# The routed experts in plain float32 matmuls on two column halves of the array, with six more weight buffers

## The chip, the cores and the metric

The kernel runs on one core of one Trainium2 chip, as one program. The metric is the device time of that core in microseconds. The core has a tensor engine (PE, with its weight loads shown apart as PEld), a vector engine (DVE), a scalar engine (ACT), a general engine (POOL), a queue that only issues transfers (SP), and 16 DMA engines. On PE a product has a stationary operand, which is loaded first, and a moving operand, which is streamed through the array column by column.

## What is computed

The reference is a network of two blocks on 512 tokens of width 1024, with a mixture of experts at its end. The change touches the experts alone. There are 32 of them, each token goes to two, and an expert is a gated layer with a hidden width of 512:

```python
N_EXPERTS = 32; TOP_K = 2; D_FF_EXPERT = 512; D_MODEL = 1024
# for every expert e, for the tokens t that the router sent to it:
xn = rms_norm(t, norm_gain)
h  = silu(xn @ w_gate[e]) * (xn @ w_up[e])      # 1024 -> 512
y  = h @ w_down[e]                               # 512 -> 1024
# a token's output: the sum over its two experts, weighted by the router
```

Everything is float32. The weights of one expert are three matrices of 2 MB, and all 32 experts are read whatever the routing says, which is 201 MB.

## The kernel before

The program is one long list of tile operations, emitted by Python methods of a class `Net` and put in order on each engine by a planner. `layer1` runs twice, then `mix2`, `cross` and `moe`. The change is in `moe`, the last phase.

Matmuls are made of a split: a float32 operand is written as a high and a low part of a reduced type (float32r), by one ACT copy and one DVE subtraction (`split`, L258 and L259), and a product is then three passes, high by high, high by low and low by high (`mm3`, L282 to L284). The expert phase does it too.

In `moe` the router fills, for each expert, a list of up to 64 tokens (`CAP`). A loop over the 32 experts then does this:

- `gather` (L1485): POOL issues an indirect transfer that brings the rows of the expert's tokens to `xg`, one token per partition. There are two `xg`, and the next expert's gather is issued an expert ahead.
- `front` (L1489): eight PE transposes of `xg` into PSUM (L1493), a DVE product with the norm's gain (`ex`), a split of that (`exh`, `exl`), and then gate and up. Each is a sum over eight blocks of 128 rows, into a bank of its own (pools `mm` and `fmm`), of which the 64 partitions of the tokens are used. The tokens are the stationary operand (128 x 64), the weights the moving one (128 x 512). ACT forms the silu, and scales by the token's 1/rms (L1511); DVE multiplies by the up part (`esg`, L1512).
- `back` (L1515), one expert behind: four transposes of `esg` (L1520), a split (`ehh`, `ehl`), and the last product into two banks `S`, one per half of the 1024 columns. ACT copies both to `ey` (L1532) and POOL issues an indirect store to `y_d` (L1533).

The weights come through `weights` (L1470): tiles of 128 x 1024 float32 (512 KB), twelve per expert, in 34 buffers named `ew` that are used in turn. SP issues the transfers (L1475) in program order. The first use of each of the first 34 buffers is held back by a tiny POOL copy (`gate`, L249), so that the loads start at five points of the phases before: ten at `first`, up to sixteen at `early`, up to 24 at `late`, up to 32 once 1/rms is there, and the last two at `ready`, when the lists are made. Each tile is then split into `ewh` and `ewl`, with three buffers each.

After the loop four tiles `ew` receive the residual by tokens (L1557), POOL builds diagonal matrices `dg`, and SP loads the experts' rows `yt` from `y_d` (L1604), which waits for the last store. The sums, the last norm and the output follow.

Of the kernel before, what the change touches and what calls it, by code (L numbers as in the profile page):

```python
# [8 lines left out]
F32 = mybir.dt.float32  # L9
# [11 lines left out]
            hh=22, hl=22, gt=10, sq=2, fw=2, fwh=2, fwl=2, yh=8, yl=8, mgh=8, mgl=8, MKH=4, MKL=4, yt=4, xt=4, ew=34, ew1=16, ew2=24, ew3=32, xgs=2, ewh=3, ewl=3, exh=2, exl=2, esg=2, ex=2, ehh=2, ehl=2, ey=3, fs=4, fo=4)  # L21
# steps of a layer of the first block, see Net.layer1
ORDER = "P0 L0 A0 V0 O0 O1 W0 K0 Q0 Q1 C0 H0 H1 H2 H3 K1 Q2 Q3 C1 H4 H5 H6 H7 R0 R1"
T = 512
# [4 lines left out]
CAP = 64  # L29
NEG = -1.0e30  # L30

# ---------------------------------------------------------------- host layout
# Constants that depend on shapes alone, and inputs rearranged (no arithmetic).
# [5 lines left out]
def _constants():  # L39
# [56 lines left out]
    # what the last phase needs comes first  # L96
# [10 lines left out]
def _masks():  # L107
    """[128, 3, 128]: causal mask, strictly earlier rows, identity; and the forget rows' selectors"""
    p = np.arange(128)
    m = np.zeros((128, 10, 128), np.float32)  # L110
    m[:, 0] = np.where(p[None, :] > p[:, None], NEG, 0.0)
    m[:, 1] = p[:, None] < p[None, :]
    for h in range(8):
        m[h, 2 + h] = 1.0
        m[32 + h, 2 + h] = 1.0
    return m
# [41 lines left out]
def _chunks(w, starts, size=128):  # L158
    """[K, N] -> per chunk [128, K/128 * size]: the blocks of a column chunk, K blocks in order."""
    k = w.shape[0] // 128  # L160
    return np.stack([w[:, s:s + size].reshape(k, 128, size).transpose(1, 0, 2).reshape(128, k * size) for s in starts])


def _flat(w, width=1024):
    """[n, 128, W] -> tiles of `width` columns of the row of blocks."""
    a = w.transpose(1, 0, 2).reshape(128, -1)
    return np.ascontiguousarray(a.reshape(128, -1, width).transpose(1, 0, 2))
# [59 lines left out]
# ---------------------------------------------------------------- the kernel  # L227


class Net:  # L230
# [3 lines left out]
    # ---- small helpers  # L234
# [4 lines left out]
    def column(self, n):  # L239
        """a few columns of their own, for the whole program"""  # L240
        self.ncol += n
        return self.cols[:, self.ncol - n:self.ncol]

    def after(self, t, gate):
        """t's first write comes after `gate` is there."""
# [8 lines left out]
    def split(self, hi, lo, src, scale=None):  # L254
        """hi + lo = src (* scale per partition), both float32r."""
# [8 lines left out]
    def wload(self, ap, width, lane=""):  # L264
        """weights in two parts; lane f: buffers of their own, for products that fill other phases' gaps"""
# [12 lines left out]
    def mm3(self, ps, wst, wmv, first, last):  # L278
        """ps += (h + l of stationary)(h + l of moving), three passes."""
# [30 lines left out]
    def wstream(self, ap, lane=""):  # L310
        """blocks [128, 128] of tiles ap[n][128, 1024] in order."""
# [7 lines left out]
    def chunk(self, stream, xs, n=512, out=None):  # L319
        """one column chunk of 128 outputs: W^T x, x a list of (hi, lo)."""  # L320
# [5 lines left out]
    # ---- norm: x * gain in two parts, and 1/rms apart  # L326
# [26 lines left out]
    def sums(self, ps, sq, ones, nb, w=1, rows=slice(0, 128)):  # L353
        """column sums of sq [.., nb * 128] by token: ps[:, (b w)] = sq_b^T ones"""
# [3 lines left out]
    def rows(self, r):  # L358
        """columns r[t, i] as rows [i, t] of a scratch in memory"""
# [11 lines left out]
    def spread_pe(self, ps, r, nb, rows=128, stride=1, at=0):  # L371
        """ps[:rows, (b t)] = r[t, b], the same in every partition"""
# [6 lines left out]
    def spread(self, out, d, nb, at=0, stride=1):  # L379
        """out[p, (b t)] = row b of d, the same in every partition"""  # L380
# [4 lines left out]
    def rsqrt(self, out, ms, scale, eps):  # L385
        """out = (ms * scale + eps) ** -0.5 on a few columns: first guess from the bits, three Newton steps."""
# [16 lines left out]
    def tokens(self, ap, ntile, kper, n, xs, rtok, nb, evac, lane=""):  # L403
        """token-major projection: out[b] [128 tokens, n], W [128, kper, n] tiles."""
# [12 lines left out]
    def half_silu(self, out, ps, rstd):  # L417
        """out = silu(ps * rstd) as (tanh(z / 2) + 1) * z / 2"""
# [6 lines left out]
    # ---- q / k heads  # L425
    def rope(self, x, cos, sin, n=512):
        """x * cos + the other half of x * sin (signed), [128 (2 heads x 64), n]"""
# [10 lines left out]
    def head_sums(self, ps):  # L438
        """mean squares of raw heads by token: sums [128, (4 blocks, 2 heads)]"""
# [6 lines left out]
    def nsa_q(self, ps, gain, cos, sin, rtok):  # L446
        """raw roped q times gain as two stacks; per token and head rstd / 8."""
# [8 lines left out]
    def head_rsqrt(self, r, ms, rtok, scale, eps):  # L456
        """rtok * (rtok^2 * ms * scale + eps) ** -0.5 for [128, (4 blocks, 2 heads)]"""
# [30 lines left out]
    def q_stack(self, x, n=512):  # L488
        """heads of rows 0-63 and 64-127 -> two [hi; lo] stacks."""
# [10 lines left out]
    def k_stack(self, x, n=512, into=None):  # L500
        """per head [hi; hi] and [lo; lo]."""
# [16 lines left out]
    # ---- softmax rows  # L518
# [16 lines left out]
    def softmax_rows(self, Ps, scores, scale=None, gate=None):  # L535
        """of the four query blocks: exp(scale * (S - max)) * gate / row sum"""
# [20 lines left out]
    def softmax(self, P, S, n, scale=None):  # L557
        """exp(scale * (S - max)), its row sum's reciprocal."""
# [11 lines left out]
    def transposed(self, Ps, causal=True, two=True):  # L570
        """P of the four query blocks -> per key block ((hi, lo) or the whole, first query column)."""
# [28 lines left out]
    def values(self, n, name, two):  # L600
        """two: per head of 64 its two parts side by side"""
# [11 lines left out]
    def pv(self, out, v, p, first, last):  # L613
        """two parts: rows 0-63 high part of v times p, rows 64-127 low part of v times the high part of p"""
# [12 lines left out]
    def out_heads(self, O, row0, hi, lo):  # L627
        """O psum [64, 512] -> rows row0.. of the chunk's hi / lo."""
# [10 lines left out]
    # ---- block 1  # L639
# [37 lines left out]
    def compress(self, l, n):  # L677
        """the compressed keys [hi; hi], [lo; lo] of [128, (g 32)], and values per head."""
# [3 lines left out]
        for i, s in enumerate("kv"):  # L682
# [10 lines left out]
            # the 32nd block does not exist: its column is never used  # L693
# [73 lines left out]
    def cmp_probs(self, l, n, g):  # L767
# [4 lines left out]
        for qb in range(4):  # L772
# [18 lines left out]
            if qb == 0:  # L791
                # queries before the first whole block see none
# [6 lines left out]
    def nsa_head(self, l, n, h, hi, lo):  # L799
        """one query head: the three branches, gated, summed in one bank."""  # L800
# [16 lines left out]
    def hgrn_proj(self, l, xs, rstd):  # L817
        """log forget gates, keys and queries of the two pairs of heads."""
# [27 lines left out]
    def hgrn_levels(self, l, r):  # L846
        """A[s, t] = sum_d q_t k_s exp(b_t - b_s), s <= t, built over halved spans, two heads at a time.

        c: sums of log f from a span's start to t; e: log k_s plus the sum after s to its span's end.
        A's block of 128 rows sb lies at column 512 * sb, from its diagonal block on."""  # L850
# [106 lines left out]
    def residual(self, w, xs, then=None, lane=""):  # L957
        """h += W^T x"""
# [67 lines left out]
    # ---- block 2  # L1026
    def rope_tables(self):
        """cos and sin of positions * frequency, over the first block's tables."""
# [24 lines left out]
    def forget_rows(self, xs, rstd):  # L1053
        """minus the cumulated log forget gate per head, hi rows 0-7 and lo rows 32-39."""
# [17 lines left out]
        # log1p(e) = log(u) + (e - (u - 1)) / u  # L1072
# [107 lines left out]
    def gates(self, i, xs, rstd, lane=""):  # L1180
        """tanh(gate / 2)"""
# [8 lines left out]
    def branch(self, i, ys, ts, out, lane=""):  # L1190
        """out(m, tanh(gate / 2), y @ w_branch)"""
# [35 lines left out]
    def memory(self, gate):  # L1227
        """keys and values of the memory."""
# [67 lines left out]
    def router_chunk(self, k):  # L1296
        """squares and logits of a chunk of the residual: the logits' rows from the unscaled tokens"""
# [7 lines left out]
        if k % 4 == 3:  # L1305
            # the residual by tokens
# [9 lines left out]
    def moe(self, out):  # L1316
        nc, tc = self.nc, self.tc
        # per place (rank * experts + expert): the token, the row of its result (2 * token + choice), the token's 1/rms
# [4 lines left out]
        # small things: `keep` for the whole phase, `once` for the routing alone  # L1323
# [37 lines left out]
        # norm, routing: logits scaled by token  # L1361
# [15 lines left out]
        def onehot(oh, v, m, down, n):  # L1377
            """first place of the maximum"""
# [19 lines left out]
        # rank of each assignment within its expert, and its row among all sorted by expert  # L1398
# [14 lines left out]
        # lists of the first round: [place, (row, 1/rms), expert], out of bounds where there is none  # L1413
# [19 lines left out]
        # weights of the two experts  # L1433
# [10 lines left out]
        # all places, for further rounds  # L1444
# [24 lines left out]
        # experts  # L1469
        def weights(ap):  # L1470
# [5 lines left out]
            wh = self.tile([128, 1024], F32R, name="ewh")  # L1476
            wl = self.tile([128, 1024], F32R, name="ewl")
            if self.nw <= CAPS["ewh"]:
                self.gate(wh, rt)
                self.gate(wl, ready)  # L1480
            self.split(wh, wl, w)
            return wh, wl
# [5 lines left out]

        def front(xg, li_e, wg, wu, pool="mm"):  # L1489
            """the tokens of one place per partition through an expert's gate"""  # L1490
# [3 lines left out]
            xh = self.tile([128, 8, CAP], F32R, name="exh")  # L1494
            xl = self.tile([128, 8, CAP], F32R, name="exl")
            f3 = "p a b -> p (a b)"
            x = self.tile([128, 8, CAP], F32, name="ex")
            self.tt(x, pt.rearrange("p (k n) -> p k n", k=8), self.p("g_ffn")[:, :, None].to_broadcast([128, 8, CAP]), OP.mult)
            self.split(xh.rearrange(f3), xl.rearrange(f3), x.rearrange(f3))
            pss = []  # L1500
            for w3 in (wg, wu):
                ps = self.mmT(pool)[:CAP]
                for t in range(4):
                    wh, wl = weights(w3[:, 2 * t:2 * t + 2, :])
                    for kk in range(2):
                        k = 2 * t + kk
                        ws = slice(kk * 512, kk * 512 + 512)
                        self.mm3(ps, (xh[:, k, :], xl[:, k, :]), (wh[:, ws], wl[:, ws]), k == 0, k == 7)
                pss.append(ps)
            sg = self.tile([CAP, 512], F32, name="esg")  # L1510
            nc.scalar.activation(sg, pss[0], AF.Silu, scale=li_e[2])  # L1511
            nc.vector.scalar_tensor_tensor(sg, pss[1], li_e[2], sg, op0=OP.mult, op1=OP.mult)  # L1512
            return sg

        def back(sg, li_e, wd):  # L1515
            """the hidden rows through an expert's last product, to their rows of y_d"""
# [181 lines left out]
```

## Time and profile before

| | us |
|---|---|
| median of 3 runs | 2651.53 |
| runs | 2646.52 to 2654.74 |
| span of the profiled execution | 2651.4 |

| engine | busy us | share of the span |
|---|---|---|
| PE | 2582.3 | 97% |
| PEld | 1862.6 | 70% |
| DVE | 1816.4 | 69% |
| ACT | 1334.6 | 50% |
| POOL | 134.4 | 5% |

The profile has the span of one execution, the busy time of each engine, and the share of time in which the 16 DMA engines had packets under way. A record of PE spans from the start of a matmul to the modelled end of its results, so neighbouring records overlap; what a matmul costs in a row of matmuls is the distance from one start to the next. A plain float32 matmul stands in the trace as two records of the full number of columns.

The expert phase takes the last quarter of the span. Its first load is issued at 1950 us, its first matmul starts at 2038.66 and its last one at 2619.37.

### The profile page before, as it was taken

Reading aid. Unit: us, or ns where it says so; the run is one execution under the profiler, and the core shown is the slowest. Engines: PE = TensorE matmul, PEld = TensorE weight load, DVE = VectorE, ACT = ScalarE, POOL = GpSimd, SP = SyncE. Lnnn points to the kernel's source line nnn. Section 1 sums busy time; section 2 is a strip of 40 time slices with the busy share of each in tenths; the row PEclk is TensorE's granted clock in tenths of the full one; section 3 lists DMA queues with packets and bytes.
Section 4 is the critical chain, followed back from the end, with each engine's and each line's share of the span. In section 5 each row is a group of like instructions: output and inputs, shape, how many; then the busy total and the mean of one; then the engine's idle time right before and its main releaser. Section 6 shows DMA issues by size and latency. Waiting matters only on the chain. (4 is left out here: it accounts for less than half of the span.)

```text
span 2651.4 us, 33625 instructions
## 1 busy us (share of the span) xinstructions
PE 2582.3 (97%) x12098; PEld 1862.6 (70%) x12099; DVE 1816.4 (69%) x3496; ACT 1334.6 (50%) x2026; POOL 134.4 (5%) x199
## 2 busy tenths in 40 slices
PE   8999999999999999999999999999997999999997
PEld 6876557888888875678888877777874555555553
DVE  6778875444346888864443378677665989888986
ACT  6544553222235445442222256554443777877784
POOL 0000000000000000000000000000011110111102
PEclk9999999999999999999999999999997999999998
DMA  5132002222231231012222231222246999999996
GB/s 199 42 106 78 9 17 90 93 95 96 96 126 58 65 118 34 1 64 95 93 92 96 95 115 56 84 92 83 92 175 237 329 342 344 338 348 350 338 344 244
DMA packets 144316, 382.32 MB, mean 144 GB/s; under 512 B 15744, under 2 KB 16144, under 8 KB 143504
## 3 DMA queue, kind: packets, MB, share of 16 engines
q1 hardware_dynamic: 138160, 369.62, 41.0%
q0 software_dynamic: 5120, 8.40, 1.0%
q10 hardware_dynamic: 864, 2.10, 0.3%
q8 instruction: 96, 1.57, 0.2%
q14 instruction: 76, 0.62, 0.1%
HBM read 370.61 MB, written 12.59 MB: 145 GB/s over the span
## 5 line engine op out<-in xcount | busy, mean ns | idle before, releaser
L258 ACT ACTIVATE wh<-w 128x1024 fp32r<-128x1024 f32 (+1 forms) x264 | 276.5, 1048 | 642.8 <-PE mm L283 352.0
L282 PE MATMUL mm<-xh,wh 128*128 128x512 f32 x1232 | 494.7, 402 | 9.9 <-ACT wh L258 9.9
L283 PE MATMUL mm<-xl,wh 128*128 128x512 f32 x1232 | 493.7, 401 | 0.0
L284 PE MATMUL mm<-xh,wl 128*128 128x512 f32 x1232 | 491.3, 399 | 0.7 <-DVE wl L259 0.7
L259 DVE TENSOR_TENSOR ewl<-ew,ewh 128x1024 fp32r<-128x1024 f32 x384 | 450.8, 1221 | 50.5 <-ACT ewh L258 48.1
L259 DVE TENSOR_TENSOR wl<-w,wh 128x1024 fp32r<-128x1024 f32 (+1 forms) x264 | 319.6, 1211 | 172.8 <-ACT wh L258 171.6
L258 ACT ACTIVATE ewh<-ew 128x1024 fp32r<-128x1024 f32 x384 | 377.8, 1047 | 14.3 <-PE mm L284 5.1
L282 PEld LDWEIGHTS mm<-xh,wh 128*128 128x128 f32 x1232 | 232.8, 189 | 66.6 <-ACT wh L258 10.0
L283 PEld LDWEIGHTS mm<-xl,wh 128*128 128x128 f32 x1232 | 232.6, 189 | 55.5 <-issue 2.9
L284 PEld LDWEIGHTS mm<-xh,wl 128*128 128x128 f32 x1232 | 232.7, 189 | 54.0 <-DVE wl L259 1.5
L252 DVE TENSOR_TENSOR tmp<-mm,xrstd 128x512 f32<-128x512 f32 x104 | 71.6, 690 | 250.6 <-PE mm L284 244.1
L283 PE MATMUL mm<-hl,wh 128*128 128x512 f32 x352 | 138.6, 394 | 0.0
L282 PE MATMUL mm<-hh,wh 128*128 128x512 f32 x352 | 138.3, 393 | 0.0
L284 PE MATMUL mm<-hh,wl 128*128 128x512 f32 x352 | 138.2, 393 | 0.0
L549 ACT ACTIVATE P<-S,st,const 128x128 f32<-128x128 f32 (+3 forms) x128 | 78.5, 616 | 52.7 <-DVE st L252 43.0
L282 PE MATMUL mm<-ewh,exh 128*64 128x512 f32 x256 | 102.0, 398 | 1.8 <-ACT exh L258 1.8
L282 PE MATMUL S<-ewh,ehh 128*64 128x512 f32 x256 | 102.4, 400 | 1.0 <-ACT ehh L258 1.0
L283 PE MATMUL mm<-ewl,exh 128*64 128x512 f32 x256 | 102.5, 400 | 0.0
L284 PE MATMUL mm<-ewh,exl 128*64 128x512 f32 x256 | 101.8, 398 | 0.4 <-DVE exl L259 0.4
L283 PE MATMUL fmm<-ewl,exh 128*64 128x512 f32 x256 | 101.6, 397 | 0.0
L282 PE MATMUL fmm<-ewh,exh 128*64 128x512 f32 x256 | 100.6, 393 | 0.5 <-ACT ewh L258 0.5
L284 PE MATMUL fmm<-ewh,exl 128*64 128x512 f32 x256 | 100.6, 393 | 0.0
(514 smaller groups left out, 4779.7 us busy)
## 6 DMA issues: line engine op xcount, KB each, us to landing
ew<-in_eg_dram SPq DMA_DIRECT2D x128, 512.0 KB
ew<-in_eu_dram SPq DMA_DIRECT2D x128, 512.0 KB
ew<-in_ed_dram SPq DMA_DIRECT2D x128, 512.0 KB
w<-in_fi_dram SPq DMA_DIRECT2D x88, 512.0 KB
w<-in_w_dram SPq DMA_DIRECT2D x48, 512.0 KB
w<-in_fo_dram SPq DMA_DIRECT2D x44, 512.0 KB
w<-in_c_dram SPq DMA_DIRECT2D x16, 512.0 KB
tmp<-tmp SPq DMA_DIRECT2D x80, 64.0 KB
```

The source lines that it names most:

```text
L252: (eng or self.nc.vector).tensor_tensor(out, a, b, op=op)
L258: nc.scalar.activation(hi, src, AF.Copy)
L259: nc.vector.tensor_tensor(lo, src, hi.bitcast(F32), op=OP.subtract)
L282: nc.tensor.matmul(ps, ah, bh, start=first, stop=False)
L283: nc.tensor.matmul(ps, ah, bl, start=False, stop=False)
L284: nc.tensor.matmul(ps, al, bh, start=False, stop=last)
L549: nc.scalar.activation(Ps[q0 + i], S[:, :n], AF.Exp, bias=b, scale=1.0 if scale is None else scale[q0 + i], accum_out=st[:, 1, i:i + 1])
```

## The change

`weights` no longer splits: it returns the loaded float32 tile. The buffers `ewh`, `ewl`, `exh`, `exl`, `ehh`, `ehl` are gone, and `ew` has 40 buffers instead of 34; the gates of the first 32 stay, and the other eight are all held by `ready`. The products are single float32 matmuls. Gate goes to partitions 0 to 63 of one bank and up to partitions 64 to 127 of the same bank, so that they stand on the two column halves of the array, and the matmuls alternate between them; the two column halves of the last product do the same. 1/rms is now applied by an ACT copy to `xg` ahead of the transposes, instead of in the silu and in the product behind it. The weights of gate and up are asked for alternately.

```diff
-            hh=22, ..., ew=34, ew1=16, ew2=24, ew3=32, xgs=2, ewh=3, ewl=3, exh=2, exl=2, esg=2, ex=2, ehh=2, ehl=2, ey=3, fs=4, fo=4)
+            hh=22, ..., ew=40, ew1=16, ew2=24, ew3=32, xgs=2, esg=2, eh=2, ex=2, ehT=2, ey=3, fs=4, fo=4)
...
             nc.sync.dma_start(w.rearrange("p (a b) -> p a b", b=ap.shape[-1]), ap)
-            wh = self.tile([128, 1024], F32R, name="ewh")
-            wl = self.tile([128, 1024], F32R, name="ewl")
-            if self.nw <= CAPS["ewh"]:
-                self.gate(wh, rt)
-                self.gate(wl, ready)
-            self.split(wh, wl, w)
-            return wh, wl
+            return w
...
+        one, two_ = slice(0, CAP), slice(CAP, 2 * CAP)
+
         def front(xg, li_e, wg, wu, pool="mm"):
+            nc.scalar.activation(xg[:CAP], xg[:CAP], AF.Copy, scale=li_e[2])
             pt = self.mmT(self.ptn)
             for k in range(8):
                 nc.tensor.transpose(pt[:, k * 64:k * 64 + 64], xg[:CAP, k * 128:k * 128 + 128], self.c("ident")[:CAP, :CAP])
...
-            self.split(xh.rearrange(f3), xl.rearrange(f3), x.rearrange(f3))
-            pss = []
-            for w3 in (wg, wu):
-                ps = self.mmT(pool)[:CAP]
-                for t in range(4):
-                    wh, wl = weights(w3[:, 2 * t:2 * t + 2, :])
-                    for kk in range(2):
-                        k = 2 * t + kk
-                        ws = slice(kk * 512, kk * 512 + 512)
-                        self.mm3(ps, (xh[:, k, :], xl[:, k, :]), (wh[:, ws], wl[:, ws]), k == 0, k == 7)
-                pss.append(ps)
-            sg = self.tile([CAP, 512], F32, name="esg")
-            nc.scalar.activation(sg, pss[0], AF.Silu, scale=li_e[2])
-            nc.vector.scalar_tensor_tensor(sg, pss[1], li_e[2], sg, op0=OP.mult, op1=OP.mult)
-            return sg
+            ps = self.mmT(pool)
+            for t in range(4):
+                ws = [weights(w3[:, 2 * t:2 * t + 2, :]) for w3 in (wg, wu)]
+                for kk in range(2):
+                    k = 2 * t + kk
+                    for r, w in zip((one, two_), ws):
+                        nc.tensor.matmul(ps[r], x[:, k, :], w[:, kk * 512:kk * 512 + 512], start=k == 0, stop=k == 7)
+            sg = self.tile([128, 512], F32, name="esg")
+            nc.scalar.activation(sg[two_], ps[one], AF.Silu)
+            h = self.tile([CAP, 512], F32, name="eh")
+            self.tt(h, ps[two_], sg[two_], OP.mult)
+            return h
...
-            self.split(hh.rearrange(f3), hl.rearrange(f3), pt[:, :256])
-            py = [self.mmT("S")[:CAP] for _ in range(2)]
+            hT = self.tile([128, 4, CAP], F32, name="ehT")
+            nc.vector.tensor_copy(hT.rearrange(f3), pt[:, :256])
+            py = self.mmT("S")
             for k in range(4):
-                wh, wl = weights(wd[:, k:k + 1, :])
-                for half in range(2):
-                    ws = slice(half * 512, half * 512 + 512)
-                    self.mm3(py[half], (hh[:, k, :], hl[:, k, :]), (wh[:, ws], wl[:, ws]), k == 0, k == 3)
+                w = weights(wd[:, k:k + 1, :])
+                for i, r in enumerate((one, two_)):
+                    nc.tensor.matmul(py[r], hT[:, k, :], w[:, i * 512:i * 512 + 512], start=k == 0, stop=k == 3)
```

The rest of the diff takes comments out.

## Rows read from the trace of the kernel before

**Rows 1.** Stretches: length, busy us of five engines, granted PE clock, DMA share, GB/s.

```profile
2019.00:2035.00 16.00, 4.13 (x46) 3.94 (x46) 9.32 (x38) 3.15 (x5) 5.81 (x21) 0.50 0.77 276
2035.00:2045.00 10.00, 8.28 (x31) 4.95 (x32) 6.63 (x8) 2.96 (x4) 3.02 (x5) 0.51 0.73 235
2045.00:2100.00 55.00, 53.02 (x242) 30.19 (x241) 48.00 (x48) 44.03 (x51) 5.48 (x5) 1.00 0.94 322
2100.00:2350.00 250.00, 250.00 (x1169) 144.52 (x1168) 224.72 (x223) 197.59 (x237) 26.23 (x28) 1.00 0.97 339
2350.00:2590.00 240.00, 240.00 (x1126) 139.02 (x1125) 215.86 (x215) 190.07 (x227) 23.40 (x25) 1.00 0.99 346
2590.00:2603.00 13.00, 13.00 (x58) 7.38 (x57) 11.73 (x12) 10.64 (x14) 6.90 (x4) 1.00 0.98 363
```

**Rows 2.** Timeline of PE, one expert: start us, us, operation, records merged.

```profile
2300.70 0.66 PE L1493 MATMUL PU<-const,xg 64*128 64x64 f32 x8
...
2303.03 0.39 PE L283 MATMUL S<-ewl,ehh 128*64 128x512 f32 x1
2303.26 0.40 PE L284 MATMUL S<-ewh,ehl 128*64 128x512 f32 x1
2303.49 0.39 PE L282 MATMUL S<-ewh,ehh 128*64 128x512 f32 x1
...
2318.70 0.66 PE L1493 MATMUL PU<-const,xg 64*128 64x64 f32 x8
```

**Rows 3.** Instructions on tile `ew`, 2100 to 2600: count, ns min/median/max, starts.

```profile
L258 ACT ACTIVATE ewh<-ew x334: 1038/1046/1057, 2099.3 to 2599.5; 128x1024 fp32r<-128x1024 f32 x167
L259 DVE TENSOR_TENSOR ewl<-ew,ewh x333: 1207/1218/1310, 2099.7 to 2599.0; 128x1024 fp32r<-128x1024 f32 x167
L1475 SPq DMA_DIRECT2D ew<-in_ed_dram x108: 327/340/1076, 2108.7 to 2597.0; - x108
L1475 SPq DMA_DIRECT2D ew<-in_eu_dram x104: 367/368/1119, 2099.8 to 2582.1; - x104
L1475 SPq DMA_DIRECT2D ew<-in_eg_dram x100: 367/378/719, 2116.4 to 2579.1; - x100
```

**Rows 4.** Timelines of SP and PE where the experts begin.

```profile
2035.71 3.66 SPq L1475 DMA_DIRECT2D ew<-in_eg_dram  x3
...
2038.66 0.66 PE L282 MATMUL mm<-ewh,exh 128*64 128x512 f32 x1 [0.69 <-ACT exh L258]
```

**Rows 5.** Timelines of SP and PE at the end of the expert phase.

```profile
2593.25 4.81 SPq L1475 DMA_DIRECT2D ew<-in_ed_dram  x6
...
2619.37 0.40 PE L284 MATMUL S<-ewh,ehl 128*64 128x512 f32 x1
...
2626.14 1.99 SPq L1604 DMA_DIRECT2D yt<-y_d  x4
```

**Rows 6.** Timeline of PE: plain float32 matmuls one after another on one half.

```profile
1980.08 0.59 PE L1285 MATMUL O<-pth,memv 128*64 128x512 f32 x1
1980.51 0.59 PE L1285 MATMUL O<-pth,memv 128*64 128x512 f32 x1
1980.94 0.59 PE L1285 MATMUL O<-pth,memv 128*64 128x512 f32 x1
```

**Rows 7.** Timelines of DVE, PE and PEld: two plain float32 matmuls on both halves.

```profile
215.31 1.06 DVE L376 TENSOR_SCALAR tmp<-const 128x128 f32<-128x128 f32 x5
...
215.73 0.63 PE L377 MATMUL X<-tmp,const 128*64 128x512 f32 x1
216.19 0.87 PE L377 MATMUL X<-tmp,const 128*64 128x512 f32 x2
216.42 0.64 PE L377 MATMUL X<-tmp,const 128*64 128x512 f32 x1
216.42 0.13 PEld L377 LDWEIGHTS X<-tmp,const 128*64 128x64 f32 x1 [0.52 <-DVE tmp L376]
216.90 0.59 PE L377 MATMUL X<-tmp,const 128*64 128x512 f32 x1
```

More of the change, by code (lines that the diff above doesn't have):

```diff
@@ L20 @@
             P=2, P2=2, pth=3, ptl=3, st=8, stc=2, r4=2, rsx=3, rsy=3, rst=3, hr=2, xtok=2, mh=8, ml=8,
-            hh=22, hl=22, gt=10, sq=2, fw=2, fwh=2, fwl=2, yh=8, yl=8, mgh=8, mgl=8, MKH=4, MKL=4, yt=4, xt=4, ew=34, ew1=16, ew2=24, ew3=32, xgs=2, ewh=3, ewl=3, exh=2, exl=2, esg=2, ex=2, ehh=2, ehl=2, ey=3, fs=4, fo=4)
+            hh=22, hl=22, gt=10, sq=2, fw=2, fwh=2, fwl=2, yh=8, yl=8, mgh=8, mgl=8, MKH=4, MKL=4, yt=4, xt=4, ew=40, ew1=16, ew2=24, ew3=32, xgs=2, esg=2, eh=2, ex=2, ehT=2, ey=3, fs=4, fo=4)
 ORDER = "P0 L0 A0 V0 O0 O1 W0 K0 Q0 Q1 C0 H0 H1 H2 H3 K1 Q2 Q3 C1 H4 H5 H6 H7 R0 R1"
@@ L1493, in front, with back @@
                 nc.tensor.transpose(pt[:, k * 64:k * 64 + 64], xg[:CAP, k * 128:k * 128 + 128], self.c("ident")[:CAP, :CAP])
-            xh = self.tile([128, 8, CAP], F32R, name="exh")
-            xl = self.tile([128, 8, CAP], F32R, name="exl")
-            f3 = "p a b -> p (a b)"
             x = self.tile([128, 8, CAP], F32, name="ex")
             self.tt(x, pt.rearrange("p (k n) -> p k n", k=8), self.p("g_ffn")[:, :, None].to_broadcast([128, 8, CAP]), OP.mult)
-            self.split(xh.rearrange(f3), xl.rearrange(f3), x.rearrange(f3))
-            pss = []
-            for w3 in (wg, wu):
-                ps = self.mmT(pool)[:CAP]
-                for t in range(4):
-                    wh, wl = weights(w3[:, 2 * t:2 * t + 2, :])
-                    for kk in range(2):
-                        k = 2 * t + kk
-                        ws = slice(kk * 512, kk * 512 + 512)
-                        self.mm3(ps, (xh[:, k, :], xl[:, k, :]), (wh[:, ws], wl[:, ws]), k == 0, k == 7)
-                pss.append(ps)
-            sg = self.tile([CAP, 512], F32, name="esg")
-            nc.scalar.activation(sg, pss[0], AF.Silu, scale=li_e[2])
-            nc.vector.scalar_tensor_tensor(sg, pss[1], li_e[2], sg, op0=OP.mult, op1=OP.mult)
-            return sg
-        def back(sg, li_e, wd):
+            ps = self.mmT(pool)
[10 more added lines that the diff above has]
+            return h
+        def back(h, li_e, wd):
             f3 = "p a b -> p (a b)"
@@ L1519, in back @@
             for k in range(4):
-                nc.tensor.transpose(pt[:, k * 64:k * 64 + 64], sg[:, k * 128:k * 128 + 128], self.c("ident")[:CAP, :CAP])
-            hh = self.tile([128, 4, CAP], F32R, name="ehh")
-            hl = self.tile([128, 4, CAP], F32R, name="ehl")
-            self.split(hh.rearrange(f3), hl.rearrange(f3), pt[:, :256])
-            py = [self.mmT("S")[:CAP] for _ in range(2)]
+                nc.tensor.transpose(pt[:, k * 64:k * 64 + 64], h[:, k * 128:k * 128 + 128], self.c("ident")[:CAP, :CAP])
+            hT = self.tile([128, 4, CAP], F32, name="ehT")
+            nc.vector.tensor_copy(hT.rearrange(f3), pt[:, :256])
+            py = self.mmT("S")
             for k in range(4):
-                wh, wl = weights(wd[:, k:k + 1, :])
-                for half in range(2):
-                    ws = slice(half * 512, half * 512 + 512)
-                    self.mm3(py[half], (hh[:, k, :], hl[:, k, :]), (wh[:, ws], wl[:, ws]), k == 0, k == 3)
+                w = weights(wd[:, k:k + 1, :])
+                for i, r in enumerate((one, two_)):
+                    nc.tensor.matmul(py[r], hT[:, k, :], w[:, i * 512:i * 512 + 512], start=k == 0, stop=k == 3)
             y = self.tile([CAP, D], F32, name="ey")
-            for half in range(2):
-                nc.scalar.activation(y[:, half * 512:half * 512 + 512], py[half], AF.Copy)
+            for i, r in enumerate((one, two_)):
+                nc.scalar.activation(y[:, i * 512:i * 512 + 512], py[r], AF.Copy)
             nc.gpsimd.indirect_dma_start(
```

## The prediction

> **What bounds the kernel now.** I read the stretches of the expert phase first [rows 1]. From 2045 us on PE is busy without a gap and has its full clock, and DVE is busy for 90% of the time. The DMA engines are as full: 97 to 99% from 2100 to 2590, at 339 to 346 GB/s. So two resources are at their limit at once, and the question is which of them is late at the end.
>
> The timeline of PE gives its pace [rows 2]: the transposes of one expert start at 2300.70 and those of the next at 2318.70, so an expert takes 18.00 us. The passes of a product start 0.23 us apart, and 72 of them are 16.56 us; the other 1.44 us are the twelve transposes and the steps around them.
>
> The instructions on the weight tiles give the pace of the transfers [rows 3]. Between 2100 and 2600 SP issued 108 + 104 + 100 = 312 tiles, while DVE split 333. A tile therefore takes the DMA engines 500 / 312 = 1.60 us and an expert's twelve 19.2 us, more than PE's 18.00. PE keeps its own pace only because the first loads were made ahead of it, and it eats some 21 tiles of that lead in this stretch. A wait view would put SP's waits down to DVE's splits; the counts speak against that, since a queue bound by freed buffers would issue as many tiles as are split.
>
> The end shows what is left [rows 5]: the last weights are issued by about 2598, and I estimate that they have landed by 2600, two tiles (3.2 us) being under way at a time. PE's last matmul starts at 2619.37 and ends at 2619.8, some 20 us later. That backlog is PE's, and it is on the path. Behind it come the copy, the store, the wait for it and the load of `yt` at 2626.14, and the end at 2651.4: 31.6 us from the last matmul to the end.
>
> The span of the profiled execution is 2651.4 us and the median of the runs 2651.53, so I take them as equal. A difference under 0.3% (8 us) can't be told from none.
>
> **Splits.** Each of the 384 tiles loses an ACT copy of 1.046 us and a DVE subtraction of 1.218 us [rows 3], 402 us and 468 us in all. PE had no gaps waiting for them [rows 1], so by itself this is worth nothing in the steady part. What it changes is that a buffer is now held until PE has read it; a split came a few us ahead of that. One price appears on the way: an ACT copy on `xg` ahead of the transposes. I bound it by the ACT copy of a whole tile, 1.05 us [rows 3], and take nothing: it lies beside the other expert's matmuls, except for the first expert, where it would cost up to that.
>
> **Matmuls.** An expert had 72 passes; it gets 24 plain float32 matmuls, which are 48 records. What a record costs is open. On one half of the array records start 0.43 us apart [rows 6]; without any overlap an expert is 48 x 0.43 + 1.44 = 22.1 us. If two halves stream at the same time, it is 24 x 0.43 + 1.44 = 11.8 us. The nearest row is a pair of float32 matmuls on the two halves, in the first block [rows 7]: starts at 215.73, 216.19, 216.42 and 216.90. The second half starts 0.23 us after the last record of the first half, not 0.43, and its own two records are 0.48 apart, no slower than the first's 0.46. So the streams do overlap. And 0.23 isn't a floor: the weight load there waited for DVE's `tmp`, which ended at 215.31 + 1.06 = 216.37. Taken literally, a matmul would cost 0.23 + 0.48 = 0.71 us and an expert 24 x 0.71 + 1.44 = 18.5 us; I take 11.8, since what held the second matmul back there is known and isn't PE, and keep 18.5 and 22.1 for the range and the rivals. The order in the queue (both records of gate, then both of up) lets the second record of one run beside the first of the next, which is one pair of records per 0.43 us.
>
> Here a rule of the Trainium skill speaks against the change. In the rows, the weight load of the second half is at 216.42, while the first half's record of 216.19 still streams (0.43 us, until 216.62) [rows 6, 7]. The page "TensorE: Matmul & The Clock Gate", Part 3, section "The mechanism", says that a weight load overlaps matmuls in flight only when its row group differs, and both halves here use all rows. By it the loads would lie between the streams; the row disagrees, so I give that a small chance, priced below.
>
> **The bound that is left.** With 11.8 us PE is faster than the transfers' 19.2, so PE follows the loads, and the time is theirs. Nothing in the change makes them faster: the same 201 MB in the same pieces. What can be saved of them is the time in which they stood still for lack of a buffer. At 2035.71 SP issues three loads over 3.66 us, where 34 buffers are used up [rows 4]; with 40 it has eight loads to issue. Six tiles are 6 x 1.60 = 9.6 us at most. From below, the idle share bounds it: against 0.98, the stretch 2035 to 2045 loses 0.25 x 10 = 2.5 us and that to 2100 loses 0.04 x 55 = 2.2 us [rows 1], 4.7 us in all; the 0.97 against 0.99 of the next 250 us is up to 5 us more. I take 7. The last weights then land at 2593.
>
> **The backlog.** When the last tile lands, two matmuls are left: three distances of 0.43 and one record of 0.59 [rows 6], 1.9 us, or about 3.5 at half the clock. I take 2.5, so PE ends at 2595.5 instead of 2619.8. The 31.6 us behind it stay: the copies, the store and the loads of `yt` are the same. The residual's four tiles, issued behind the last weights, now land some 6 us (four tiles) after 2593; the store needs longer than that (the last matmul's end to the issue of `yt` is 6.3 us [rows 5]), so they are hidden, by a hair.
>
> The sum: 2651.4 - 7 (buffers) - 17.3 (backlog, 19.8 less 2.5) = 2627.1, so 2627 us.
>
> **Clock.** With PE at 11.8 of 19.2 us it has short pauses, and may not keep its clock: in the routing it was busy for 4.13 of 16 us and the granted clock was 0.50, the 1.2 GHz level [rows 1]. At that level an expert is about 23.6 us, more than the loads. But then PE has no pauses, and the rows show that it climbs back when it works without them (0.51, then 1.00) [rows 1]. So I price it as a backlog at the end only: one expert at half clock, 23.6 - 19.2 = 4 us, against nothing. It is in the range.
>
> **Rivals.**
> - The halves overlap poorly, and PE stays late. The end is 2651.4 + 32 x (p - 18.00), with p the time of an expert on PE. With the literal 0.71 us it is 2667; without any overlap 32 x 4.1 = 131 us more, 2782. This is the case that ends slower; it decides from 0.70 us per float32 matmul on (p = 18.25). For it: no row shows a long stream on both halves. Against it: the start at 216.42 [rows 7].
> - Weight loads of one half don't run beside matmuls of the other: each of 48 loads (0.13 us [rows 7]) stands between, 11.8 + 6.2 = 18.0 us, and the time is 2651, no change. This is the page's rule from above, and the same row speaks against it.
> - The transfers become faster, since loads no longer stand still for buffers and two engines stop reading the tiles. The last stretch ran at 363 GB/s [rows 1]; at that rate 312 tiles take 500 x 343 / 363 = 472 us, 28 us less, and the time would be 2599. Against it: that stretch has mostly tiles of the last product and the residual, and the share was 0.97 to 0.99 with 339 to 346 GB/s for 490 us.
> - The buffers bring nothing and PE's clock is low at the end: 2627 + 7 + 6 = 2640.
>
> **How the numbers follow.** The forecast, bound by the transfers with the halves overlapping, 2612 to 2643 (the ends of the buffers' and the backlog's terms, the low clock among them): 73%. Overlap so poor that PE stays late: 15%, of which 6% stay within the rows' 0.69 to 0.70 us or gain a little (2644 to 2659) and 9% are slower. Weight loads in between: 4%, mostly no change. Faster transfers: 5%. Anything else, such as a stall at the residual's tiles: 3%, slower. The range that leaves out less than two in ten is 2600 to 2652. Faster by over 0.3% (below 2643.5): 0.78. Within: 0.09. Slower: 0.13.
>
> **What the profile after would show.** Right: the split's rows are gone; the two matmuls of a pair start far less than 0.86 us apart; an expert takes about 19 us; PE has idle time that ends with transfers of `ew`, the DMA share stays at 0.97 to 0.99 from about 2045 on, and the last matmul is within 3 us of the last weights. Wrong: PE without gaps and an expert of over 18 us on it, or a GB/s that differs from 340 to 350 by more than a few per cent, or a last stretch longer than 31.6 us.

## The result, and the profile after

The changed kernel takes 2696.85 us (median of 4 runs, 2694.48 to 2698.82), the kernel before 2649.03 us in the same comparison (2646.11 to 2654.74). The ratio is 1.0172, with a 95% interval of 1.0152 to 1.0191: slower by 1.7%, where 0.9% faster was forecast. The profiled execution has a span of 2695.7 us.

The stretches of the expert phase, with the columns of [rows 1] (length, busy us of PE, PEld, DVE, ACT and POOL, granted PE clock, DMA share, GB/s):

```profile
2035.00:2045.00 10.00, 9.72 (x35) 3.20 (x35) 0.69 (x1) 2.43 (x3) 0.96 (x1) 0.69 0.86 295
2045.00:2100.00 55.00, 53.97 (x285) 22.26 (x282) 9.21 (x16) 13.11 (x19) 8.70 (x10) 1.00 0.97 339
2100.00:2350.00 250.00, 197.62 (x758) 57.44 (x758) 24.64 (x41) 36.41 (x50) 24.37 (x26) 0.96 0.88 309
2350.00:2590.00 240.00, 186.58 (x664) 51.37 (x664) 19.90 (x33) 32.11 (x44) 19.62 (x21) 0.94 0.86 303
```

PE has gaps now, as forecast, but the transfers have gaps too: 0.86 to 0.88 and 303 to 309 GB/s, where 0.97 to 0.99 and 339 to 346 stood before [rows 1]. Between 2045 and 2100 PE uses up the tiles loaded ahead; from then on neither side is full.

The tile `esg` is written once per expert, so its instructions give the pace (name, count, ns min/median/max, first to last start; every second expert is in such a row):

```profile
L1501 ACT ACTIVATE esg<-mm x6: 588/588/589, 2151.7 to 2364.9; 64x512 f32<-64x512 f32 x6
```

Ten experts in 2364.9 - 2151.7 = 213.2 us are 21.3 us each; before it was 18.00 [rows 2].

The waits tell who holds whom, for 2100 to 2500 (who waits, line, for what: us in total, times, longest):

```profile
SPq L1475 <- DVE eh L252: 102.7, 20, 10.8
SPq L1475 <- PE S L1518: 57.8, 14, 5.7
SPq L1475 <- PE fmm L1499: 54.3, 6, 9.4
SPq L1475 <- PE mm L1499: 27.1, 3, 9.2
SPq L1475 <- PE PU L1511: 19.3, 19, 6.6
```

```profile
PE S L1518 <- DMA ew<-in_ed_dram: 26.9, 22, 2.6
PE mm L1499 <- DMA ew<-in_eu_dram: 14.4, 32, 1.5
PE fmm L1499 <- DMA ew<-in_eu_dram: 14.3, 34, 1.9
```

PE waits for loads, and SP, which issues the loads in order, waits for PE and for what follows from PE's newest results, 261 of 400 us. `DVE eh` and `PE PU` are two halves of one wait: a load that has to follow the transposes of `eh` waits first for `eh` itself. One such circle, in the timelines of SP, then of PE (start us, us, operation, records merged):

```profile
2202.86 15.10 SPq L1475 DMA_DIRECT2D ew<-in_ed_dram  x4
2218.00 0.43 SPq L1475 DMA_DIRECT2D ew<-in_eg_dram  x1
2218.48 0.47 SPq L1475 DMA_DIRECT2D ew<-in_eu_dram  x1
2222.49 0.37 SPq L1475 DMA_DIRECT2D ew<-in_eg_dram  x1
```

```profile
2217.14 0.46 PE L1511 MATMUL PU<-const,eh 64*128 64x64 f32 x4 [0.55 <-DVE eh L252]
2221.36 1.08 PE L1518 MATMUL S<-ew,ehT 128*64 128x512 f32 x4 [1.11 <-DMA ew<-in_ed_dram]
```

The last of four `ed` loads goes out only when the transposes of `eh` end (2217.14 + 0.46 = 2217.60). PE then stands 1.11 us for that very tile, and the next held `eg` load goes out at 2222.49, when the last product's matmul on it has ended (2222.44). Seven loads go out within 3.3 us then, and the same begins again.

The built program says why. The planner doesn't keep the weight tiles in 40 slots; it places each tile wherever memory has come free, and the tiles of the phase rotate over 58 places, among them those of `ex`, `eh`, `esg` and `ehT`. Counted in the program's waits, 58 of the loads after the 60th may not go out before all but two of the tiles ahead of them are used up by PE, because they land where the newest `ex`, `eh` or `ehT` was just read. In the trace 24 of the 58 are released by the transposes, which read `eh`, 19 by the last product, which reads `ehT`, 14 by gate and up, which read `ex`, and one by the product `eh`. Theory A is that these holds, with the loads queued behind each, are the whole loss.

The end, in the timeline of SP, then of PE:

```profile
2633.08 22.77 SPq L1475 DMA_DIRECT2D ew<-in_ed_dram  x8
...
2671.64 2.15 SPq L1593 DMA_DIRECT2D yt<-y_d  x4
```

```profile
2658.66 2.37 PE L1518 MATMUL S<-ew,ehT 128*64 128x512 f32 x8 [0.24 <-DMA ew<-in_ed_dram]
```

PE ends 2.4 us after its last wait for a load, at 2661.0, and the rest, to the end of the span, takes 34.7 us.

### The profile page after: what moved, and what is told of

Same layout as the page of the kernel before. It is cut to its first block, busy times and chain, and to the rows that moved or that the text cites. A ratio compares the mean times of both kernels' runs of the same rounds, so it can differ in the third digit from the quotient of the medians.

```text
span 2695.7 us, 30462 instructions
## 1 busy us (share of the span) xinstructions
PE 2502.8 (93%) x11330; PEld 1674.8 (62%) x11331; DVE 1355.8 (50%) x3080; ACT 969.7 (36%) x1610; POOL 123.8 (5%) x199
## 5 line engine op out<-in xcount | busy, mean ns | idle before, releaser
L1499 PE MATMUL fmm<-ew,ex 128*64 128x512 f32 x512 | 168.4, 637 | 33.0 <-DMA ew<-in_eu_dram 23.3
L1499 PE MATMUL mm<-ew,ex 128*64 128x512 f32 x512 | 169.6, 657 | 30.4 <-DMA ew<-in_eu_dram 18.7
L1518 PE MATMUL S<-ew,ehT 128*64 128x512 f32 x512 | 149.0, 639 | 44.3 <-DMA ew<-in_ed_dram 43.4
L1499 PEld LDWEIGHTS mm<-ew,ex 128*64 128x64 f32 x512 | 44.9, 147 | 156.2 <-issue 66.6
L1499 PEld LDWEIGHTS fmm<-ew,ex 128*64 128x64 f32 x512 | 44.0, 141 | 155.3 <-DMA ew<-in_eu_dram 70.7
L252 DVE TENSOR_TENSOR eh<-fmm,esg 64x512 f32<-64x512 f32 x16 | 11.1, 693 | 222.0 <-ACT esg L1501 222.0
L252 DVE TENSOR_TENSOR eh<-mm,esg 64x512 f32<-64x512 f32 x16 | 11.1, 693 | 218.9 <-ACT esg L1501 218.8
L1521 ACT ACTIVATE ey<-S 64x512 f32<-64x512 f32 x64 | 37.8, 590 | 180.4 <-PE S L1518 168.5
L1518 PEld LDWEIGHTS S<-ew,ehT 128*64 128x64 f32 x512 | 32.3, 139 | 101.5 <-DMA ew<-in_ed_dram 72.5
```

What stands on the lines that cost most here:

```text
L252: (eng or self.nc.vector).tensor_tensor(out, a, b, op=op)
L1499: nc.tensor.matmul(ps[r], x[:, k, :], w[:, kk * 512:kk * 512 + 512], start=k == 0, stop=k == 7)
L1518: nc.tensor.matmul(py[r], hT[:, k, :], w[:, i * 512:i * 512 + 512], start=k == 0, stop=k == 3)
L1521: nc.scalar.activation(y[:, i * 512:i * 512 + 512], py[r], AF.Copy)
```

## The experiments

The rivals to theory A: B, the transfers themselves became slower, since PE now reads the loaded float32 tiles; C, TensorE's own work is the bound; and later D, the order of loads and matmuls, or the places, and not the waits.

**ring38: the weight tiles in 38 fixed buffers.**

```diff
+            if len(ring) == 38:
+                w = ring[self.nw % 38]
+                self.nw += 1
+                nc.sync.dma_start(w.rearrange("p (a b) -> p a b", b=ap.shape[-1]), ap)
+                return w
             w = self.tile([128, 1024], F32, name="ew")
+            ring.append(w)
```

> The changed kernel, but the experts' weight tiles are 38 fixed buffers used in turn, so a load waits only for the matmuls on the tile 38 places earlier and never for memory that ex, eh, esg or ehT have just left. Theory A (about three loads per expert land on memory of the current expert's small tiles, SP issues in order, so all loads behind are held): between 2100 and 2590 us the DMA share returns from 0.86-0.88 to 0.95 or more and 335-350 GB/s, PE's idle time before its expert matmuls still ends with loads, and the time is 2615 to 2635 us. Rival B (the transfers themselves have become slower, because PE now reads the loaded float32 tiles itself): 300 to 312 GB/s stay, time 2680 to 2700 us. Rival C (TensorE's own work is the bound, halves that overlap badly): PE busy over 97% of the stretch, time over 2670 us.

Measured: 2582.96 us (2579.55 to 2583.89), 0.9733 of before, interval 0.9713 to 0.9753: faster than before by 2.7%, and than the changed kernel by 114 us. The stretch, SP's largest waits in 2100 to 2500, and the time of the loads from issue to landing there:

```profile
2100.00:2350.00 250.00, 217.41 (x919) 70.95 (x916) 28.31 (x48) 45.31 (x62) 29.02 (x31) 0.99 1.04 379
```

```profile
SPq L1476 <- DMA ew<-in_eu_dram: 96.7, 89, 2.8
SPq L1476 <- DMA ew<-in_eg_dram: 94.8, 91, 2.2
SPq L1476 <- DMA ew<-in_ed_dram: 68.6, 92, 1.6
```

```profile
DMA to landing us min/median/max: 10.2/11.6/13.2
```

B and C fall: the same float32 tiles, read by the same matmuls, arrive at 379 GB/s, and PE still waits for them. The size surprised: A had 335 to 350 GB/s and 2615 to 2635 us. The share goes to 1.04, so 0.97 to 0.99 was not full. SP now waits almost only for the landing of earlier loads, 260 of its 282 us; at 17.4 us per expert (below), 1.45 us per tile, a landing of 11.6 us means eight loads under way, as many as the program has semaphores (counters that tell of a landing) for them. In the changed kernel the same view gives

```profile
DMA to landing us min/median/max: 3.5/8.1/12.8
```

that is, a queue that runs from full to empty and back. Counted in the traces from issue to landing, between 2100 and 2500 us, ring38 has seven or eight loads under way at all times, the changed kernel 0 to 8, on average 4.3, and the kernel before 1 to 6, on average 3.8.

**ring38_one_half: the same on one column half.** `ps` and `py` become two tiles `[:CAP]` each, and all matmuls write rows 0 to 63.

> As ring38, but gate and up, and the two halves of the last product, all go to the lower column half, each in its own PSUM bank. If the two column halves run side by side in the changed kernel: TensorE needs 24+... 48 records of 0.43 us, about 22 us per expert instead of about 12, is the bound, and the time is 2740 to 2790 us. If they do not overlap, the time is that of ring38.

Measured: 2779.57 us. This is one run. The halves run side by side; without that, even with the ring, the kernel would be 5% slower than before. The pace:

```profile
L1509 ACT ACTIVATE esg<-fmm x6: 590/590/591, 2160.0 to 2379.8; 64x512 f32<-64x512 f32 x6
```

219.8 / 10 = 21.98 us per expert; the prediction had 22.1 for no overlap.

**after_ew34: the six buffers taken back.** `ew=40` to `ew=34`, nothing else.

> The changed kernel with 34 weight buffers as before instead of 40. Theory A: the tiles get the same addresses as with 40, and the same loads wait for the same small tiles; within 0.3% of the changed kernel (2690 to 2705 us). If the six more buffers matter by what the prediction gave them: 2704 us. If the six buffers are what pushed the tiles onto the small tiles' memory: back under 2660 us.

Measured: 2695.24 us (2 runs), the changed kernel's time. The six buffers don't cause the holds, and no gain from them shows.

**before_ring34: fixed buffers in the kernel before.** The ring as above, with the split kept.

> The kernel before (split and three passes), with its 34 weight buffers fixed and used in turn. Theory A: its transfers were already 97 to 99% busy, so little is there to win: 2635 to 2652 us, share 0.97 or more. If before lost time in the same way as the changed kernel, it falls below 2630 us.

Measured: 2667.17 us, ratio 1.0056, interval 1.0036 to 1.0076; slower than both expectations. The loads run faster (352 GB/s against 339 [rows 1]), which buys nothing: PE was the bound. PE now waits 24 times between 2100 and 2540 us, once per expert, for ACT's copy `ehh`, which stands behind the split of a weight tile; in the kernel before, PE has no such wait there. The stretch, then PE's wait:

```profile
2100.00:2350.00 250.00, 241.71 (x1131) 139.18 (x1130) 221.16 (x217) 195.67 (x230) 25.25 (x27) 1.00 0.99 352
```

```profile
PE S L282 <- ACT ehh L258: 14.2, 24, 0.6
```

That is 0.59 us per expert, 19 us over 32, more than the 13 us lost.

**ring38_held: one wait per expert put back.**

```diff
+                if self.nw % 12 == 0 and hts:
+                    nc.vector.tensor_copy(w[:, :1], hts[-1][:, 0, :1])
```

> ring38 with one wait put back: before the first gate tile of each expert is loaded, VectorE copies one column of the newest ehT into that buffer, so that one load in twelve, and with it all loads behind it on SP, has to wait for the expert just computed. Nothing else changes; the transfers and TensorE's work are those of ring38 (2583 us). Theory A (loads held behind one load): the rate between 2100 and 2500 us falls from 380 GB/s to 290 to 350, SP's longest wait is on that copy, PE waits for loads again, and the time is 2640 to 2710 us. Rival D (ring38 gained through the changed order of SP's loads and of PE's work, not through the missing waits): it stays within 10 us of 2583.

Measured: 2588.44 us, 5 us more than ring38, where A expected 2640 to 2710 and D within 10 us of 2583. The stretch and SP's only wait on the copy (2000 to 2500 us):

```profile
2100.00:2350.00 250.00, 221.14 (x902) 70.98 (x902) 30.44 (x63) 44.73 (x61) 29.02 (x31) 0.99 1.04 382
```

```profile
SPq L1478 <- DVE ew L1476: 12.9, 1, 12.9
```

As it stood, A missed here, and D gained. But the wait bound only once: in the steady part SP is eight tiles ahead, and by then `ehT` is written. What might count is how few tiles are left when a load may go.

**ring38_no_load: TensorE alone.** In the ring's branch the `dma_start` is taken out, so the later experts compute with what lies in the buffers.

> ring38 without the loads after the first 38: every later expert computes with what lies in the buffers (that part of the computation is changed). It shows TensorE's own price of one expert without transfers. By the prediction's working 11.8 us per expert, so the time is 2440 to 2480 us; if the two column halves overlapped worse, 14 us or more per expert, over 2520 us.

Measured: 2437.80 us (one run). One expert in PE's timeline:

```profile
2154.07 0.46 PE L1518 MATMUL PU<-const,eh 64*128 64x64 f32 x4
...
2158.59 7.07 PE L1506 MATMUL fmm<-ew,ex 128*64 128x512 f32 x32
2165.58 0.46 PE L1518 MATMUL PU<-const,eh 64*128 64x64 f32 x4
```

11.51 us per expert, and 32 records in 7.07 us: two per 0.44 us.

**ring8: eight buffers.** 38 becomes 8.

> ring38 with 8 buffers in place of 38, so that at most 8 tiles are in flight or in use, and fewer in flight than ring38's. If the rate of the loads hangs on how many are in flight: clearly below ring38's 380 GB/s between 2100 and 2500 us, 300 to 350, and with the lost head start of 30 tiles the time is 2670 to 2740 us. If the rate is a property of the float32 tiles or of the port alone: 375 to 385 GB/s stay and the time is about 2583 + 30 x 1.38 = 2624 us.

Measured: 2622.40 us (one run), and 372 to 384 GB/s:

```profile
2100.00:2350.00 250.00, 214.69 (x847) 67.01 (x848) 25.34 (x42) 42.01 (x57) 26.16 (x28) 1.00 1.04 374
```

Eight buffers in a regular ring keep the transfers fuller than 40 that the planner places. Thirty more bring only the head start: (2622.4 - 2583.0) / 30 = 1.3 us each.

**ring42: four more.** 38 becomes 42.

> ring38 with 42 buffers. The stretch is bound by transfers of 1.38 us per tile, so each further buffer that is loaded ahead of the first matmul is worth up to 1.38 us: 2577 to 2583 us. If the loads ahead are limited by something else (the time between the routing and the first matmul), no change: 2583 us.

Measured: 2584.74 us (2582.16 to 2587.30): no change from ring38. The loads ahead are limited there by something else; by what was not tried.

**ring38_tight3 and ring38_tight6: two loads per expert that take a buffer just used.**

```diff
-                w = ring[self.nw % 38]
+                w = ring[(self.nw - {7: 3, 10: 6}.get(self.nw % 12, 0)) % 38]    # tight3
+                w = ring[(self.nw - 6 * (self.nw % 12 in (7, 10))) % 38]         # tight6
```

> ring38, but the loads at places 7 and 10 of each twelve take the buffer of the tile 3 places earlier, as loads of the changed kernel take memory that was read just before: they can't be issued until all but two of the tiles ahead of them are used up (50 loads; the changed kernel has 58 such among its loads after the 60th). All else is ring38 (2583 us). ring38_held put a wait where it bound little, since eight loads are ahead there anyway. Theory A: the changed kernel lost 2697 - 2583 = 114 us on 58 such loads, about 2.0 us each, so 50 cost about 98 us: 2660 to 2695 us, with 300 to 325 GB/s and PE waiting for loads. Rival D (order of SP's loads and of PE's work, or the places in memory, not the waits): within 10 us of 2583.

> As ring38_tight3, but with the buffer of the tile 6 places earlier: 51 loads wait until five tiles are left. Theory A: five tiles last PE longer than the 3.5 us that a lone load takes to land, so the queue does not run dry: 2583 to 2600 us. If any wait of this kind costs by itself: as ring38_tight3.

Measured: tight3 2659.46 us (5 runs, 2657.32 to 2673.86), tight6 2589.80 us (2 runs). Stretches of tight3, then of tight6:

```profile
2100.00:2350.00 250.00, 206.49 (x797) 60.75 (x797) 23.52 (x39) 39.10 (x53) 24.33 (x26) 1.00 0.93 332
```

```profile
2100.00:2350.00 250.00, 223.06 (x906) 70.78 (x902) 28.26 (x47) 44.72 (x61) 29.01 (x31) 1.00 1.04 378
```

D falls: the same loads in the same ring cost 76 us when they go out with two tiles left, 1.5 us per held load, and 7 us in all with five left. A's 2.0 us per load was too much by a third, and tight3 ends 1 us under A's range.

**after_own_small: the changed kernel with only its small tiles in memory of their own.** `ex`, `esg`, `eh`, `ehT` and `ey` are two tiles each, made once ahead of the loop and used in turn; the planner still places the weights.

> The changed kernel with only its small tiles (ex, esg, eh, ehT, ey) put into memory of their own for the whole phase; the weight tiles are still placed by the planner. The loads now reuse other weight tiles, and each waits until 4 to 38 tiles are left, never for the last two. Theory A: most of ring38's gain, 2585 to 2610 us, 365 GB/s or more. If the gain needs the fixed ring (its regular order): 2640 us or more.

Measured: 2586.84 us (2 runs), 0.9765 of before, with 379 to 382 GB/s:

```profile
2100.00:2350.00 250.00, 219.96 (x883) 69.26 (x880) 26.44 (x44) 44.14 (x60) 28.06 (x30) 0.99 1.04 379
```

The ring isn't needed: keeping the loads off the small tiles' memory gives all but 4 us of what it gives.

**ring38_all_held: the changed kernel's own list of held loads.**

```diff
+                at = held[self.nw] = held[self.nw - HOLD[self.nw] - 1] if self.nw in HOLD else self.nw % 38
+                w = ring[at]
```

> ring38 with the changed kernel's own list of held loads: each of its 69 waiting loads from the 60th on takes the buffer of a tile as many places back as it has in the changed kernel (58 of them two tiles from the end). From the 139th load on, SP's order and the waits are those of the changed kernel, 49 loads held at two tiles, 2.4 per expert against 2 in ring38_tight3; before that SP issues other loads ahead of the held ones, so the first 90 us run nearer to ring38's pace. Theory A with the holds as the whole cause: between 2350 and 2500 us the same rate as the changed kernel (306 GB/s, 300 to 312) and about 0.33 us more per tile than ring38 on 245 tiles, 2583 + 80 = 2663 us (2655 to 2685). If something else in the changed kernel (places in memory) took the rest of its loss: 320 GB/s or more there, and no more than ring38_tight3's 2659 us.

Measured: 2686.31 us (2680.86 and 2691.76), the profiled execution 2679.2. Its stretches, then those of the changed kernel:

```profile
2230.00:2350.00 120.00, 91.89 (x344) 25.76 (x344) 10.86 (x18) 17.41 (x24) 11.22 (x12) 0.99 0.89 309
2350.00:2500.00 150.00, 118.60 (x431) 34.30 (x432) 12.67 (x21) 20.32 (x28) 13.08 (x14) 0.95 0.91 321
2500.00:2600.00 100.00, 78.57 (x289) 22.59 (x286) 9.05 (x15) 12.19 (x18) 7.43 (x8) 0.95 0.84 298
```

```profile
2230.00:2350.00 120.00, 92.04 (x343) 25.99 (x344) 10.86 (x18) 15.18 (x21) 10.29 (x11) 0.96 0.87 307
2350.00:2500.00 150.00, 118.39 (x420) 32.30 (x420) 12.67 (x21) 20.44 (x28) 13.08 (x14) 0.94 0.87 306
2500.00:2600.00 100.00, 76.93 (x266) 21.45 (x267) 7.24 (x12) 12.86 (x18) 7.46 (x8) 0.91 0.86 302
```

The verdict is mixed. Between 2350 and 2500 us, where A expected 300 to 312 GB/s, it has 321, the rival's rate; on either side it has 309 and 298, the changed kernel's. The time is 1 us over A's range and 27 over the rival's. Put back into ring38, the holds make up 103 of the 114 us. The remaining 11 us are no more than the distance of the two runs here, so they may be noise; if they are real, their cause (first loads that are held less tightly here, the clock, or places in memory) stays open. The granted clock fell to 0.95 with the holds, as in the changed kernel, and was 1.00 in tight3. What that costs wasn't measured by itself and is part of the 103 us: at tight3's 1.5 us per load, 58 held loads would cost 89.

## Why the prediction was wrong

**TensorE's part was right.** 11.8 us per expert were forecast with overlapping halves, and ring38_no_load has 11.51; without overlap 22.1, and ring38_one_half has 21.98. Taking the pair of [rows 7] as an overlap and not at its literal 0.71 us was the right choice. With weight loads between the streams the prediction had estimated an expert at 18.0 us, from its rows. The rule behind that, of the Trainium skill (page "TensorE: Matmul & The Clock Gate", Part 3, "The mechanism"), that weight loads overlap matmuls in flight only across row groups, doesn't hold for the column halves here, since an expert took 11.51.

**The backlog** was right in kind, and PE ends 2.4 us after its last wait for a load, where 2.5 were forecast. But it was never 19.8 us: by the updates of the loads' semaphores, the last weight tile of the kernel before landed at 2605.6 and not at 2600, since at 2598 five tiles were still under way and not two. The backlog was 14.2 us.

**"Nothing in the change makes them faster" is the step that failed.** It took 19.2 us per expert as a property of the transfers, since their share was 0.97 to 0.99, and let them keep that pace. That share isn't a ceiling: the same loads ran at 1.04 and 380 GB/s as soon as nothing held them, and ring38's pace is

```profile
L1509 ACT ACTIVATE esg<-fmm x7: 588/588/589, 2157.6 to 2366.6; 64x512 f32<-64x512 f32 x7
```

209.0 / 12 = 17.4 us. What set the pace of the loads before was SP's waits. The prediction named that view and set it aside, because a queue bound by freed buffers would issue as many tiles as are split. The row itself, of the kernel before in 2100 to 2500, was

```profile
SPq L1475 <- DVE ewl L259: 287.7, 221, 5.1
```

288 of 400 us. The counting argument assumes that a split tile's slot goes to the next load. With a planner that places by address this is false: a load can wait for a tile that is split late while the memory of tiles split before it lies free. The built program of the kernel before shows it. Slots used in turn would let every load go with 33 loaded tiles still to be split; by the program's waits the loads around the 40th may go with 32 left, around the 200th with 21, around the 330th with 12. These 20 tiles are the lead that the prediction saw PE eat and put down to slow transfers. So the pace of the loads was a result of the plan, and the change made a new plan. I held the transfers constant; they went from 19.2 to 21.3 us per expert, and PE's last wait for a load ends at 2658.7, where the forecast had the last load at 2593.

**The buffers were mis-sized**: -7 us forecast, no gain measured (after_ew34). "34 buffers are used up" treated the tiles as slots of their own; the holds came from the small tiles' memory, which no term of the sum contained. The sentence that a buffer "is now held until PE has read it" saw the direction and left out the queue: one held load stops all loads behind it.

**The last stretch** was 31.6 us and became 34.7. The residual's tiles were to be "hidden, by a hair"; the load of `yt` now goes out 10.6 us after the last matmul (2661.0 to 2671.64) instead of 6.3 [rows 5]. The last store, on POOL, did stand 0.96 us for a residual tile; that the residual's loads are behind the rest is only argued.

**The clock** was priced as a backlog at the end, 4 us. It was low over the whole phase, 0.94 to 0.96 from 2100 to 2590 us. Since the held loads wait for PE's work, a slower PE holds them longer; how much that cost isn't measured.

**Settled up**, against 2651.4 and with the prediction's own 2600 and 19.8: last load +58.7, backlog -17.4, last stretch +3.1: 2695.8, and the span is 2695.7. With the landing at 2605.6 the first two terms are 5.6 us smaller each, and the sum is the same.

**The rivals.** The slower side was expected mostly from poor overlap, which didn't occur; no rival let the loads become slower. "Faster transfers" (363 GB/s, 2599 us) was nearer to what the change can give: 2583 with ring38. Of the signs named for a wrong prediction two showed: the GB/s outside 340 to 350 (303 to 309), and a last stretch longer than 31.6 us (34.7).

## What to carry to other kernels

Ask of a stream of loads not how busy the transfers are but what its queue waits for, and how many tiles are left when that wait ends: two loads per expert held with two tiles left cost 76 us, with five left 7. Where a planner places tiles by address, a change of tile shapes makes a new plan of waits; give streamed tiles, or the small ones between them, memory of their own, and count waits in the built program before forecasting. Buffers beyond what the queue holds buy only the head start, 1.3 us each from 8 to 38 here and nothing from 38 to 42.

## What the runs showed of the hardware

- The share of the DMA engines read 0.97 to 0.99 at 339 to 346 GB/s and 1.03 to 1.04 at 372 to 385: a share near one left 10% of the rate. In the kernel before, 3.8 loads of 512 KB were under way on average at the first, in ring38 seven or eight at the second.
- Plain float32 matmuls on two column halves run fully side by side: two records per 0.44 us (7.07 us for 32), an expert in 11.51 us against 21.98 on one half.
- Two streams of matmuls that both wait for loads were granted different clocks: 0.94 to 0.96 from 2100 to 2590 us in the changed kernel (a mean of the levels 2.4 GHz, read as 1.00, and 1.2, read as 0.50), 1.00 in ring38_tight3. PE's longest waits for loads were 2.6 us in the one and 1.9 in the other.
